# Tying the splits of the output projection's attention rows behind chosen exponentials and masked sums

## The chip, the cores and the metric

The kernel runs on one core of a Trainium2 chip. The metric is device time in microseconds (us) of one execution; several executions are timed and their median is taken. One more execution is taken by the hardware profiler, and all durations of single instructions come from it.

## What is computed

One block of a streaming encoder on 1024 rows of width 1024, all in float32: a SwiGLU feed-forward with a layer norm, a mixer with a layer norm, a second feed-forward with a layer norm. Cut to what matters here, the mixer:

```python
fox = forgetting_attention(q, k, v, fg)            # 8 heads of width 64, blocks of 128 queries
lru = gelu(z_lg) * rg_lru(conv(z_lx))              # 512 recurrent channels
mix = concat([fox, lru], -1) @ w_out               # 512 attention rows and 512 recurrent rows of w_out
x   = layer_norm(ALPHA * x + mix)
# attention, of each head and each block i of 128 queries, on the keys up to the diagonal:
s = q_i @ k.T * scale + cum[queries] - cum[keys];  s = where(mask, s, -1e30);  p = softmax(s);  o_i = p @ v
```

## The kernel before

A float32 matrix product is done in three passes: each operand is split into a high part in the format fp32r and a low part, the rest, and `mm3` (lines 156 to 158) adds high x high, high x low and low x high. A split is a cast by ScalarE (the high part) and a subtraction by VectorE (source minus high part).

The program is written with a framework that takes the instructions in program order with their dependencies and then chooses each engine's order itself: an instruction that is ready and has its buffers can be put ahead of earlier ones that are not ready. `issue_behind(later, earlier)` and `issue_after` give it an order to keep: `later` may not be put ahead of `earlier` on their common engine. Such a tie adds no semaphore.

The attention (`attention`, with `probs`, `to_pT` and `values`) runs over a list of 64 units, a unit being a head and a block i of 128 queries. Heads 0 to 5 go one after another, blocks 7 down to 0; the 16 units of heads 6 and 7 are interleaved, in the order (6,7) (6,6) (6,5) (6,4) (7,7) (7,6) (6,3) (6,2) and so on. So unit 40 is (5,7), unit 47 is (5,0), unit 48 is (6,7), unit 49 (6,6), unit 51 (6,4) and unit 53 (7,6). In the profile a unit is known by the width of its exponential, 128 x (i + 1) columns. For unit n:

- `probs`: the scores by TensorE (lines 999 and 1000) into one of two score buffers; GpSimd masks the diagonal of the `cum` tile (line 1003); VectorE adds `cum` and takes the minimum over the row in one instruction, the masked sum (line 1005); ScalarE takes the exponential (line 1006), which also adds up the row. For heads 0 to 3 the row is then divided by its sum (lines 1008 and 1009).
- `to_pT` of an earlier unit (three units back in the first four heads, two in the others): TensorE transposes the exponentials (line 1020), ScalarE and VectorE split them (lines 1024 and 1025).
- `values`, one unit later still, for each pair of blocks: TensorE multiplies by v (line 1041), ScalarE and VectorE take the result out (lines 1044 and 1045), and after the second head of a pair it is scaled (lines 1050 and 1051) and split into the mix tiles (lines 1053 and 1054).

Between the units stands other work. The recurrent half of the output projection, sixteen tiles of 12 matmuls (`fill`), goes into units 0 to 35. The attention half is done by the output tiles (`out_tile`), from unit 56 on, each of 12 matmuls and every second one followed by the layer norm of its rows; they need the mix tiles of four pairs of heads and the four split rows of `w_out`. These splits are made by the generator `out_w`, one for each `next(w_steps)`, and kept in `w_fox`. It loads two row blocks into one `raw` tile, then splits each by `split_ws` (lines 148 and 149). The parts go into `ws` tiles, eight buffers, which the splits of the recurrent rows hold before. The `raw` tiles have two buffers; after the attention the first weights of the second feed-forward take them (line 264, on SyncE's queue, where the loads of heads, of stored mix tiles (line 1110) and of the layer norm's two rows stand as well). The first use of those weights is at line 319.

Of the kernel before, what the change touches and what calls it, by code (L numbers as in the profile page):

```python
# [12 lines left out]
AF = mybir.ActivationFunctionType  # L13
ALU = mybir.AluOpType
# [34 lines left out]
def f32(ap):  # L49
    return ap.bitcast(F32)  # L50


class Block:
# [91 lines left out]
    def split_ws(self, src, k):  # L145

        hi, lo = (self.wsp.tile([P, 4 * VW], F32R, tag="ws", name=self.nm("w"))[:, 0:D].rearrange("p (k c) -> p k c", k=k) for _ in range(2))
        self.nc.scalar.copy(hi, src)
        self.nc.vector.tensor_tensor(lo, src, f32(hi), ALU.subtract)
        return hi, lo  # L150

    def mm3(self, out, lhs, rhs, first, last, goes_on=False):
# [810 lines left out]
    def attention(self, w_out, mixp, ln, normed):  # L963

        nc, v = self.nc, self.nc.vector
# [5 lines left out]
        with self.pool("att_p", 3) as pp, self.pool("att_t", 1) as tp, self.pool("att_pt", 6) as ptp, self.pool("att_qk", 2, side="right") as qkp:  # L971

            def load(h):
                vt = qkp.tile([P, NT, P], F32R, tag="v", name=self.nm("v"))
                cum = qkp.tile([P, T], F32, tag="cum", name=self.nm("cum"))
                q, kh, kl = (qkp.tile([P, T], F32R, tag=t, name=self.nm(t)) for t in ("q", "kh", "kl"))
                mine = slice(64 * (h % 2), 64 * (h % 2) + 64)
                for j in range(2):
                    rows = slice(64 * j, 64 * j + 64)
                    nc.sync.dma_start(f32(q[rows]), self.q_d[h // 2, j, mine, :])  # L980
                    nc.sync.dma_start(f32(kh[rows]), self.k_d[h // 2, 0, mine, :])
                    nc.sync.dma_start(f32(kl[rows]), self.k_d[h // 2, 1, mine, :])
                row = self.cum_d[h:h + 1, :]
                nc.sync.dma_start(cum, bass.AP(tensor=row.tensor, offset=row.offset, ap=[[0, P], [1, T]]))
                self.last_load = nc.sync.dma_start(f32(vt), self.v_d[h].rearrange("(j p) d -> p j d", p=P))
                return q, kh, kl, vt, cum

            sums, inv = self.fgz, self.wf.rearrange("p h i -> p (h i)").rearrange("p (h i) -> p h i", h=HEADS)

            def probs(h, i):  # L990

                q, kh, kl, _, cum = heads[h]
                n = (i + 1) * P
                ts = slice(i * P, n)
                s = self.s_tile()
                for bank in range((n + H - 1) // H):
                    c1 = min(max(n - bank * H, 256), H)
                    cols = slice(bank * H, bank * H + c1)
                    mm(s[:, bank, 0:c1], q[:, ts], kh[:, cols], start=True, stop=False)
                    scores = mm(s[:, bank, 0:c1], q[:, ts], kl[:, cols], start=False, stop=True)  # L1000
                sf = s.rearrange("p b c -> p (b c)")
                p = pp.tile([P, T], F32, tag="p", name=self.nm("p"))
                nc.gpsimd.affine_select(cum[:, ts], cum[:, ts], pattern=[[-1, P]], compare_op=ALU.is_ge, fill=1e30, base=0, channel_multiplier=1)
                m = self.small.tile([P, 4], F32, tag="m", name=self.nm("m"))
                v.tensor_tensor_reduce(p[:, 0:n], sf[:, 0:n], cum[:, 0:n], 1.0, 3e38, ALU.add, ALU.min, m[:, 1:2])
                nc.scalar.activation(p[:, 0:n], p[:, 0:n], AF.Exp, bias=m[:, 1:2], scale=-1.0, accum_out=sums[:, h, i:i + 1])
                if h < LAST:
                    v.reciprocal(m[:, 3:4], sums[:, h, i:i + 1])
                    nc.gpsimd.tensor_scalar(p[:, 0:n], p[:, 0:n], m[:, 3:4], 1.0, op0=ALU.mult, op1=ALU.mult)
                return p, scores  # L1010

            def to_pT(h, i, p):
                if i % 2:
                    pts[h, i // 2] = [tuple(ptp.tile([P, 4, 256], F32R, tag="pt", name=self.nm("pt")) for _ in range(2))
                                      for _ in range((i + 4) // 4)]
                for g in range((i + 4) // 4):
                    js = range(4 * g, min(4 * g + 4, i + 1))
                    pa = self.a_tile()
                    for j in js:
                        nc.tensor.transpose(pa[:, (j % 4) * P:(j % 4 + 1) * P], p[:, j * P:(j + 1) * P], self.ident)  # L1020
                    w = len(js)
                    pav = pa.rearrange("p (j t) -> p j t", j=4)[:, 0:w, :]
                    hi, lo = (x[:, 0:w, (i % 2) * P:(i % 2 + 1) * P] for x in pts[h, i // 2][g])
                    nc.scalar.copy(hi, pav)
                    v.tensor_tensor(lo, pav, f32(hi), ALU.subtract)
                if h > LAST and h % 2 and i % 2 == 0:
                    r = inv[:, h - 1:h + 1, i:i + 2]
                    v.reciprocal(r, sums[:, h - 1:h + 1, i:i + 2])
                    nc.gpsimd.tensor_copy(self.gate_raw.rearrange("p u (b d) -> p u b d", b=2),
                                          r.rearrange("p b u -> p u b").unsqueeze(3).to_broadcast([P, 2, 2, 64]))  # L1030
# [28 lines left out]
            heads, pts, ps, outs, mixes = {}, {}, {}, {}, {}  # L1059
# [9 lines left out]
            def due(n):  # L1069

                return [u for u in (n - AHEAD, n - AHEAD + 1) if 0 <= u < len(units) and u + AHEAD - (u >= LAST * NT) == n]
# [3 lines left out]
            def out_tile():  # L1075
                i, d = tiles.pop(0)
                self.down_tile(i, list(zip(mix + [mixes[3]], w_fox)), 1.0, (d,))
                if d:
                    self.layer_norm(i)
                    normed(i)  # L1080

            for n in range(len(units) + AHEAD + 1):
                if n < len(units):
                    h, i = units[n]
                    if i == 5 and h < 6 or (h, i) == (6, 6):
                        heads[h + 1] = load(h + 1)
                    if i == NT - 1:
                        if h % 2 == 0:
                            outs[h // 2] = tp.tile([P, T], F32, tag="o", name=self.nm("o"))
                        else:  # L1090
                            mixes[h // 2] = tuple(mixp.tile([P, T], F32R, tag="h", name=self.nm("mix")) for _ in range(2))
                    ps[n], scores = probs(h, i)
                for m in due(n):
                    to_pT(*units[m], ps.pop(m))
                for m in due(n - 1):
                    h, i = units[m]
                    if i % 2 == 0:
                        values(h, i // 2)
                        if h == HEADS - 1:
                            tiles += [(i + 1, 0), (i + 1, 1), (i, 0), (i, 1)]  # L1100
                if fill and (n < 2 or n % 8 in (2, 3, 4)):
                    i, d = fill.pop(0)
                    with self.tc.issue_after(scores.ins) if n < 3 else nullcontext():
                        self.down_tile(i, lru_tiles, 1.0, (d,))
                if 45 <= n < 53 and n % 2:
                    w_fox.append(next(w_steps))
                if n in MIXES:
                    mix.append(tuple(self.hp.tile([P, T], F32R, tag="h", name=self.nm("mix")) for _ in range(2)))
                    for l in range(2):
                        nc.sync.dma_start(f32(mix[-1][l]), mix_d[len(mix) - 1][l])  # L1110
                    if len(mix) == 3:
                        self.load_gb(*ln, [self.hp.tile([P, T], F32, tag="h", name=self.nm("gb")) for _ in range(2)])
                if tiles:
                    out_tile()
# [136 lines left out]
```

## Time and profile before

| what | value |
|---|---|
| median of three runs | 2323.7 us (2322.83 to 2324.29) |
| profiled execution, time | 2323.84 us |
| profiled execution, span | 2322.1 us |
| TensorE matmul, busy | 2302.8 us |
| VectorE, busy | 1631.8 us |
| ScalarE, busy | 1012.6 us |
| granted TensorE clock, mean | 0.999 |
| first and last exponential of the attention, start | 1184.5 and 1358.4 us |

Times in the profile are us from the start of the span. PE is TensorE (PEld its weight loads), DVE is VectorE, ACT is ScalarE, POOL is GpSimd, SPq the queue of DMA issues on SyncE. A line such as L1006 is line 1006 of the kernel before. In a time line the columns are start, duration, engine, line, operation, output and input by the program's names, shapes, count, and in brackets the idle time of the engine just before it and what ended it. In a row of instruction groups the three numbers are the shortest, the median and the longest duration in ns.

### The profile page before, as it was taken

How to read it: one execution, taken by the hardware profiler on the slowest of the kernel's cores; microseconds unless marked ns; L12 is line 12 of the kernel's file. 1: busy time of each engine (PE TensorE's matmuls, PEld its weight loads, DVE VectorE, ACT ScalarE, POOL GpSimd, SP SyncE). 2: the span in 40 equal slices, each digit the busy share in tenths (PEclk: the TensorE clock that was granted, in tenths of full speed). 3: DMA queues.
4: the chain of work that ended last, by engine and by line, in shares of the span. 5: the costliest groups of instructions: out<-in, count | busy, mean ns of one | idle time of the engine just before them, and what ended most of it. 6: DMA issues, size and time to landing. Idle time of an engine off the chain costs nothing.

```text
span 2322.1 us, 28275 instructions
## 1 busy us (share of the span) xinstructions
PE 2302.8 (99%) x10737; PEld 1916.8 (83%) x10737; DVE 1631.8 (70%) x2489; ACT 1012.6 (44%) x1589; POOL 202.7 (9%) x344
## 2 busy tenths in 40 slices
PE   9999999999999999999999999999999999999998
PEld 7888888888888888888898787888888888888887
DVE  8766566666567788866667899665656665577886
ACT  5443333333344335454456745434333333344342
POOL 0020000000000000111133200000000000000000
PEclk9999999999999999999999999999999999999999
DMA  4333232323375433132275812232323232564542
GB/s 145 129 94 119 87 118 87 118 87 118 125 265 200 163 127 120 65 103 96 101 203 146 245 64 94 88 118 88 122 93 124 87 118 87 193 246 169 182 144 73
DMA packets 175976, 298.93 MB, mean 129 GB/s; under 512 B 8208, under 2 KB 100688, under 8 KB 175840
## 3 DMA queue, kind: packets, MB, share of 16 engines
q1 hardware_dynamic: 152768, 218.16, 28.9%
q0 software_dynamic: 23072, 78.97, 8.6%
q8 instruction: 84, 1.38, 0.2%
q14 instruction: 52, 0.43, 0.1%
HBM read 214.22 MB, written 82.87 MB: 128 GB/s over the span
## 4 chain that ended last, share of the span: by engine, by line
PE 93%; DVE 4%; ACT 1%; DMA 1%; issue 1%; SPq 0%; DVEq 0%; ACTq 0%
PE x L156 9%; PE x L158 9%; PE x L157 9%; PE b L156 7%; PE b L157 7%; PE b L158 7%; PE s L157 6%; PE s L158 6%; PE s L156 6%; PE a L158 6%; PE a L156 6%; PE a L157 6%; PE a L1041 1%; PE a L1020 1%; PE a L898 1%
## 5 line engine op out<-in xcount | busy, mean ns | idle before, releaser
L283 ACT CAST ws<-t 128x512 fp32r<-128x512 f32 x240 | 149.1, 623 | 394.6 <-PE b L157 267.3
L283 ACT CAST ws<-raw 128x512 fp32r<-128x512 f32 x180 | 112.0, 623 | 258.2 <-PE x L157 256.8
L284 DVE TENSOR_TENSOR ws<-raw,ws 128x512 fp32r<-128x512 f32 x180 | 123.9, 688 | 141.3 <-ACT ws L283 137.9
L284 DVE TENSOR_TENSOR ws<-t,ws 128x512 fp32r<-128x512 f32 x240 | 164.5, 686 | 70.4 <-ACT ws L283 68.5
L156 PE MATMUL b<-As,ws 128*128 128x512 f32 x512 | 199.6, 390 | 0.8 <-ACT row L517 0.4
L157 PE MATMUL a<-ws,ws 128*128 128x512 f32 x512 | 199.6, 390 | 0.2
L156 PE MATMUL a<-ws,ws 128*128 128x512 f32 x512 | 199.3, 390 | 0.5 <-ACT row L526 0.5
L157 PE MATMUL b<-As,ws 128*128 128x512 f32 x512 | 199.5, 390 | 0.0
L156 PE MATMUL x<-As,ws 128*128 128x512 f32 x512 | 199.3, 389 | 0.0
L158 PE MATMUL b<-As,ws 128*128 128x512 f32 x512 | 199.3, 389 | 0.0
L158 PE MATMUL a<-ws,ws 128*128 128x512 f32 x512 | 199.2, 389 | 0.0
L158 PE MATMUL x<-As,ws 128*128 128x512 f32 x512 | 199.2, 389 | 0.0
L157 PE MATMUL x<-As,ws 128*128 128x512 f32 x512 | 199.2, 389 | 0.0
L156 PE MATMUL x<-A,ws 128*128 128x512 f32 x496 | 193.3, 390 | 0.1
L158 PE MATMUL x<-A,ws 128*128 128x512 f32 x496 | 193.1, 389 | 0.0
L157 PE MATMUL x<-A,ws 128*128 128x512 f32 x496 | 193.0, 389 | 0.0
L621 ACT CAST ws<-raw 128x1024 fp32r<-128x1024 f32 x112 | 117.4, 1050 | 159.3 <-PE a L157 88.1
L624 DVE TENSOR_TENSOR ws<-raw,ws 128x1024 fp32r<-128x1024 f32 x112 | 136.6, 1221 | 53.0 <-ACT ws L621 52.5
L556 POOL DMA_DIRECT2D h_d<-row x96 | 68.8, 719 | 1147.2 <-DVE row L550 1108.1
L156 PE MATMUL s<-ws,ws 128*128 128x512 f32 x384 | 149.5, 389 | 0.0
L158 PE MATMUL s<-ws,ws 128*128 128x512 f32 x384 | 149.4, 389 | 0.0
L157 PE MATMUL s<-ws,ws 128*128 128x512 f32 x384 | 149.4, 389 | 0.0
(255 smaller groups left out, 5210.5 us busy)
## 6 DMA issues: line engine op xcount, KB each, us to landing
raw<-h_d SPq DMA_DIRECT2D x56, 1024.0 KB, 5.4
h_d<-row POOLq DMA_DIRECT2D x96, 512.0 KB, 3.4
wd<-in_ffn_w_down_dram SPq DMA_DIRECT2D x32, 1024.0 KB, 7.6
raw<-in_ffn_w_gate_dram SPq DMA_DIRECT2D x30, 1024.0 KB, 5.1
raw<-in_ffn_w_up_dram SPq DMA_DIRECT2D x30, 1024.0 KB, 5.2
h_d<-row POOLq DMA_DIRECT2D x32, 256.0 KB, 2.4
raw<-in_w_in_dram SPq DMA_DIRECT2D x16, 512.0 KB, 4.7
row<-in_x_dram SPq DMA_DIRECT2D x12, 512.0 KB, 8.4
```

What stands on the lines that cost most here:

```text
L156: mm(out, ah, bh, start=first, stop=False, skip_group_check=goes_on)
L157: mm(out, ah, bl, start=False, stop=False, skip_group_check=goes_on)
L158: mm(out, al, bh, start=False, stop=last, skip_group_check=goes_on)
L283: nc.scalar.copy(hi, src)
L284: v.tensor_tensor(lo, src, f32(hi), ALU.subtract)
L556: nc.gpsimd.dma_start(d[:, 2 * n:2 * n + 2], t.rearrange("p (r t) -> p r t", r=2))
L621: cast = nc.scalar.copy(hi, src)
L624: self.mark = v.tensor_tensor(lo, src, f32(hi), ALU.subtract)
L898: nc.tensor.matmul(pa[:, 0:width], xh, wh[:, 0:width], start=k == 0, stop=False)
L1020: nc.tensor.transpose(pa[:, (j % 4) * P:(j % 4 + 1) * P], p[:, j * P:(j + 1) * P], self.ident)
L1041: mm(pv[:, ps], vt[:, j, :], pts[h, qt][j // 4][l][:, j % 4, ps], start=j == 0 and l == 0, stop=j == last and l == 1)
```

## The change

The splits of the attention rows of `w_out` are asked for two units later, at units 47, 49, 51 and 53 instead of 45, 47, 49 and 51. And each is given two ties: its cast goes behind the exponential of that unit on ScalarE, its subtraction behind the masked sum of that unit on VectorE. For that, `split_ws` keeps its two instructions, and `probs` returns the exponential and the masked sum.

```diff
     def split_ws(self, src, k):
...
-        self.nc.scalar.copy(hi, src)
-        self.nc.vector.tensor_tensor(lo, src, f32(hi), ALU.subtract)
+        self.split_ops = (self.nc.scalar.copy(hi, src),
+                          self.nc.vector.tensor_tensor(lo, src, f32(hi), ALU.subtract))
...
-                v.tensor_tensor_reduce(p[:, 0:n], sf[:, 0:n], cum[:, 0:n], 1.0, 3e38, ALU.add, ALU.min, m[:, 1:2])
-                nc.scalar.activation(p[:, 0:n], p[:, 0:n], AF.Exp, bias=m[:, 1:2], scale=-1.0, accum_out=sums[:, h, i:i + 1])
+                low = v.tensor_tensor_reduce(p[:, 0:n], sf[:, 0:n], cum[:, 0:n], 1.0, 3e38, ALU.add, ALU.min, m[:, 1:2])
+                exp = nc.scalar.activation(p[:, 0:n], p[:, 0:n], AF.Exp, bias=m[:, 1:2], scale=-1.0, accum_out=sums[:, h, i:i + 1])
...
-                return p, scores
+                return p, scores, (exp, low)
...
-                    ps[n], scores = probs(h, i)
+                    ps[n], scores, ops = probs(h, i)
...
-                if 45 <= n < 53 and n % 2:
+                if 47 <= n < 55 and n % 2:
                     w_fox.append(next(w_steps))
+                    for part, op in zip(self.split_ops, ops):
+                        self.issue_behind(part, op)
```

## The prediction

> **What bounds the kernel now.** I read the page first, then a table of busy time by stretch through attention, the chain that ended last around the four splits, the time lines of TensorE, ScalarE and VectorE there, and last SyncE's queue and the uses of the raw tiles.
>
> ```profile
> span 2322.1 us, 28275 instructions
> PE 2302.8 (99%) x10737; PEld 1916.8 (83%) x10737; DVE 1631.8 (70%) x2489; ACT 1012.6 (44%) x1589; POOL 202.7 (9%) x344
> ...
> PE 93%; DVE 4%; ACT 1%; DMA 1%; issue 1%; SPq 0%; DVEq 0%; ACTq 0%
> ```
>
> TensorE is the bound of the whole. Only 7% of the chain lies off it, so a change on ScalarE and VectorE can matter only where TensorE waits for them. The next table is of the stretches that the splits leave and enter.
>
> ```profile
> core 0: us, PE busy (x) PEld busy (x) DVE busy (x) ACT busy (x) POOL busy (x), PEclk, DMA share, GB/s
> 1271.30:1281.50 10.20, 10.19 (x58) 8.75 (x59) 9.27 (x19) 9.13 (x19) 1.83 (x6) 1.00 0.62 153
> 1281.50:1292.45 10.95, 10.20 (x75) 9.09 (x73) 10.36 (x24) 8.18 (x20) 1.74 (x5) 1.00 0.82 286
> 1292.45:1308.30 15.85, 14.79 (x97) 11.82 (x96) 14.38 (x38) 13.10 (x34) 5.09 (x12) 1.00 0.98 246
> 1308.30:1328.60 20.30, 19.41 (x137) 16.38 (x137) 18.49 (x42) 17.42 (x40) 6.80 (x17) 1.00 0.92 290
> 1328.60:1345.00 16.40, 16.03 (x88) 13.20 (x87) 13.43 (x31) 8.49 (x19) 2.71 (x6) 1.00 0.25 96
> ```
>
> The first stretch still holds matmuls of the recurrent rows, which fill TensorE (10.19 of 10.20 us). They end at 1281.5 us. The first output tile starts at 1328.6 us. Between the two TensorE has attention alone, and VectorE is busy 10.36 of 10.95, 14.38 of 15.85 and 18.49 of 20.30 us (95, 91 and 91%): it is the engine that sets the pace there. From 1328.6 us TensorE is covered again and VectorE has air (13.43 of 16.40). The granted clock is 1.00 in every stretch, so no part of the argument hangs on it.
>
> **Where the splits stand now.** First the rows of the two split lines in this stretch and the shares of the chain from 1279.5 to 1289 us, then ScalarE's time line, then TensorE's.
>
> ```profile
> L148 ACT CAST w<-raw x4: 1046/1050/1061, 1279.6 to 1288.3; 128x1024 fp32r<-128x1024 f32 x4
> L149 DVE TENSOR_TENSOR w<-raw,w x4: 1217/1220/1226, 1280.7 to 1293.8; 128x1024 fp32r<-128x1024 f32 x4
> by line: ACT w L148 32.4%; ACT p L1006 14.3%; DVE w L149 12.9%; ACT pt L1024 11.3%; issue 10.8%; ACT o L1044 7.7%; DVE row L222 7.3%; DVE p L1005 6.3%; DVE mix L1054 3.5%; DVE m L1005 0.2%; ACTq L1006 0.2%; DVEq L1005 0.0%
> ```
>
> ```profile
> 1284.65 1.05 ACT L148 CAST w<-raw 128x1024 fp32r<-128x1024 f32 x1
> 1285.72 0.37 ACT L1044 COPY o<-a 64x256 f32<-64x256 f32 x1
> 1286.11 0.58 ACT L1024 CAST pt<-a 128x512 fp32r<-128x512 f32 x1
> ```
>
> ```profile
> 1285.71 0.65 PE L1020 MATMUL a<-ident,p 128*128 128x128 f32 x4
> 1286.75 0.39 PE L1041 MATMUL a<-pt,v 128*128 128x256 f32 x1 [0.39 <-ACT pt L1024]
> ...
> 1289.88 0.48 PE L999 MATMUL s<-kh,q 128*128 128x512 f32 x1
> 1290.72 0.39 PE L1041 MATMUL a<-pt,v 128*128 128x256 f32 x1 [0.37 <-ACT pt L1024]
> ...
> 1293.14 0.28 PE L1000 MATMUL s<-kl,q 128*128 128x256 f32 x1
> 1293.79 1.09 PE L1020 MATMUL a<-ident,p 128*128 128x128 f32 x8 [0.37 <-ACT p L1006]
> ```
>
> The program asks for the splits at units 45 to 51, but the scheduler has put all four casts between 1279.6 and 1288.3 us, among units 35 to 40, as soon as the weight buffers of the recurrent rows come free. In that stretch 32.4% and 12.9% of the chain, some 4.3 of 9.5 us, are splits. The reader should see the cast of 1284.65 (1.05 us) with the copy and the cast of line 1024 queued behind it on ScalarE, and TensorE waiting for that last one at 1286.75; the second wait follows the last split cast (1288.3) in the same way, the third follows the subtractions that delay unit 40's masked sum.
>
> **The change part by part.** No instruction is added or dropped: the same 4 casts and 4 subtractions, the same two loads of the raw rows. Keeping the two handles in `split_ws` and returning them from `probs` issues nothing. The ties carry no semaphore; they fix order on one engine. What moves:
>
> (1) *The early stretch is freed.* The lost TensorE time is the start of the stalled matmul less the start before it and its pitch. The pitches are estimates from the rows above: 0.11 us for a transpose (four in 0.65, less a tail of 0.2), 0.12 and 0.23 for 256 and 512 columns (durations of 0.28 and 0.39 less the same overlap of about 0.16). So 1286.75 - 1285.71 - 0.44 = 0.60; 1290.72 - 1289.88 - 0.23 = 0.61; 1293.79 - 1293.14 - 0.12 = 0.53. Together 1.74 us, and since each follows a split I take all of it as given back. The ends are 0 (VectorE's other load sets the pace and a new wait takes the place of each) and 2.05 us (the 1.74 and 0.1 for each restart of the weight pipeline).
>
> (2) *The late stretch is loaded.* Unit 47 is the last of head 5, 49 the second of head 6, 51 the fourth, 53 the second of head 7. The first and the last of their exponentials, and the long gaps of VectorE behind them:
>
> ```profile
> 1304.95 0.40 ACT L1006 ACTIVATE p<-p,m 128x128 f32<-128x128 f32 x1
> ...
> 1321.24 1.05 ACT L1006 ACTIVATE p<-p,m 128x896 f32<-128x896 f32 x1 [0.22 <-DVE m L1005]
> ```
>
> ```profile
> 1306.56 0.42 DVE L1045 TENSOR_TENSOR o<-o,a 64x256 f32<-64x256 f32 x1 [0.76 <-ACT o L1044]
> ...
> 1319.78 0.41 DVE L1045 TENSOR_TENSOR o<-o,a 64x256 f32<-64x256 f32 x1 [0.77 <-ACT o L1044]
> ...
> 1329.44 0.18 DVE L1028 RECIPROCAL wfr<-fgz 128x4 f32<-128x4 f32 x1 [1.05 <-ACT p L1006]
> ```
>
> A split can start at the earliest behind these, so all four land between 1305.3 and about 1325 us, in the stretches with VectorE at 91%. Four subtractions are 4 x 1.22 = 4.88 us of VectorE. The casts run on ScalarE beside that, so they are not added again. Behind a subtraction the next unit's masked sum is queued, and behind that the exponential, the transposes and the release of the score banks. The three long gaps, 0.76 + 0.77 + 1.05 = 2.58 us, can swallow part: 4.88 - 2.58 = 2.3 us, which I take, because in the early stretch, with splits in it, VectorE's idle time is down to 10.95 - 10.36 = 0.59 us, so gaps do get filled. The ends are 0 (the subtractions run while TensorE has its own work) and 4.88 (they meet no gap).
>
> (3) *Who waits for the weights.* The first output tile starts at 1328.6 us and takes them in order, and the last split is done at about 1321.24 + 1.05 + 1.05 + 1.22 = 1324.6 us: 4 us early. Nothing; were the cover gone, TensorE would wait at line 156.
>
> (4) *SyncE's queue.* The raw tiles are two buffers, and the next to use them are the first weights of the second feed-forward block.
>
> ```profile
> 1313.37 0.46 SPq L264 DMA_DIRECT2D raw<-in_ffn_w_up_dram  x1
> ...
> 1321.69 1.56 SPq L1110 DMA_DIRECT2D mix<-mix_d  x2
> L319 ACT CAST ws<-raw x4: 603/618/624, 1369.8 to 1389.1; 128x512 fp32r<-128x512 f32 x4
> DMA to landing us min/median/max: 4.9/6.1/9.3
> ```
>
> The gate loads now wait for split 2 and the up loads for split 4 (1324.6 instead of 1313.4, 11 us later). With 9.3 us to landing that is 1334 us, 36 us before the first use at 1369.8. Cost nothing, unless the up load stands in the queue ahead of the mix pair now at 1321.69: a rival below. The two loads of the raw output rows are asked for two units later, long before use: nothing.
>
> The sum: -1.74 + 2.3 = +0.56, so +0.6 us. Against the profiled execution (2323.84 us with a span of 2322.1) 2324.4; the median of the three runs, 2323.7, lies 0.14 below that execution, so 2324.3. What a measurement of this kernel can tell from no change is about 0.2%, 4.65 us.
>
> **A lock between VectorE and GpSimd.** The subtraction's two inputs are both in SBUF, and the trace shows what that does:
>
> ```profile
> 1293.81 1.22 DVE L149 TENSOR_TENSOR w<-raw,w 128x1024 fp32r<-128x1024 f32 x1
> 1293.96 1.22 POOL L1003 TENSOR_SCALAR_AFFINE_SELECT cum<-cum 128x128 f32<-128x128 f32 x1 [1.20 <-DVE m L1005]
> L1003 POOL TENSOR_SCALAR_AFFINE_SELECT cum<-cum x53: 283/292/1221, 1200.7 to 1332.8; 128x128 f32<-128x128 f32 x53
> ```
>
> The mask of the next unit took 1.22 instead of 0.292 us, and ended at 1295.18, 0.15 us behind the subtraction. A mask starts when the masked sum before it is done, the very instruction behind which the subtractions are now tied, so all four may hold one: 4 x 0.15 = 0.6 us more on the way to the next masked sum. The Trainium skill, "SBUF — State Buffer", section "Who interferes with whom", has the rule: a VectorE instruction with two SBUF inputs and a GpSimd instruction that reads SBUF exclude each other for the whole instruction. By that rule the sum would be +1.2 us; the trace agrees in the one overlap it shows, by 1.22 against 0.292.
>
> **The rivals.** *The gain is kept* (33%): the subtractions fall into gaps, term (2) goes to 0, and 2323.7 - 1.74 gives 2322.0, down to 2321.65. For it: the early splits are on the chain, and the late stretch has the 2.58 us of gaps. Against: two of the three gaps end when ScalarE's copy comes, and a cast put in front of that copy makes the gap longer instead of filling it.
>
> *VectorE pays in full* (7%): each subtraction stands between two masked sums, no gap is met, and a wait comes back early for each one removed: 4.88 + 0.6 = +5.5, 2329.2 us, slower by 0.24%. It decides as soon as the subtractions start right where VectorE has other work ready and TensorE's score banks are both taken. For it: VectorE at 91% in that stretch and TensorE's waits there on masked sums. Against: 1.74 us of early waits can hardly all return.
>
> *The mix pair waits in SyncE's queue* (5%): if the up load is ordered first, the pair goes out at 1324.6 + 0.46 instead of 1321.69, 3.4 us later. It decides only past the slack, the third weight of the first tile, some 2 us behind 1328.6; so +0.6 + 1.4 at the worst, 2325.7 us, and with the normalisation's two rows, which go out behind the pair, up to the whole 3.4, 2327.7 us. Against: the queue's order is chosen with the buffers' release known.
>
> *The ties change nothing* (3%): not possible by order, since the units they name run at 1305 us and later; only the splits going even further back, under the output tiles, would give 2322.0 to 2323.7.
>
> **How the numbers follow.** The forecast, 2324.3, has 52%, with a range of its own from 2323.0 to 2326.3 (a late cost of 1.0 to 4.3 against the same 1.74). The range over all cases is 2321.5 to 2327.5: it takes in the kept gain and the queue's rival nearly whole and leaves out the full price. Faster by over 0.2% would need more than the 2.05 us bound: 2%. Slower by over 0.2% needs the full price or a large part of it beside the queue: 5%. Within 0.2%: 93%.
>
> **What would show it.** Right if the casts and subtractions of the split lie at 1305 to 1326 us in the profile after, the waits at 1286, 1290 and 1293 shrink or go, and TensorE's waits on masked sums between 1305 and 1328 grow; the first output tile should then start within 1 us of 1328.6. Term (1) is wrong if unit 40's exponential still starts at 1292.5; term (2) if the stretch from head 6's first exponential to the first output tile keeps its 20.3 us. Wrong altogether if the scheduler reorders the attention units around the freed places, so that their order on TensorE no longer compares.

## The result, and the profile after

The changed kernel takes 2327.8 us (median of 20 runs, 2326.1 to 2331.06) against 2323.57 us before (20 runs, 2321.94 to 2325.7): ratio 1.0019, 95% interval 1.0013 to 1.0025. It is slower by 4.2 us. The profiled execution took 2328.62 us with a span of 2326.9 us.

The page of the profile after, its span, engines and chain; below it, the table by stretch for the same five stretches as before.

```profile
span 2326.9 us, 28267 instructions
...
PE 2302.3 (99%) x10737; PEld 1915.4 (82%) x10737; DVE 1631.8 (70%) x2489; ACT 1012.6 (44%) x1589; POOL 203.1 (9%) x344
...
PE 92%; DVE 4%; DMA 1%; ACT 1%; issue 1%; SPq 0%; POOL 0%; DVEq 0%; POOLq 0%; ACTq 0%
```

```profile
1271.30:1281.50 10.20, 10.20 (x60) 8.62 (x59) 8.60 (x19) 7.10 (x16) 2.02 (x6) 1.00 0.60 152
1281.50:1292.45 10.95, 10.94 (x80) 9.81 (x79) 8.73 (x23) 7.65 (x22) 1.66 (x6) 1.00 0.82 290
1292.45:1308.30 15.85, 13.36 (x91) 11.06 (x90) 12.68 (x33) 12.26 (x30) 4.58 (x11) 1.00 1.05 254
1308.30:1328.60 20.30, 17.16 (x114) 13.69 (x113) 18.81 (x37) 18.05 (x37) 6.73 (x14) 1.00 0.75 238
1328.60:1345.00 16.40, 14.50 (x83) 11.95 (x82) 11.85 (x31) 7.76 (x18) 2.86 (x7) 1.00 0.31 107
```

TensorE's work is the same (2302.3 against 2302.8 us), so the whole loss is idle time of TensorE. In the second stretch it is now busy 10.94 instead of 10.20 us, in the last three 13.36, 17.16 and 14.50 instead of 14.79, 19.41 and 16.03. To see where, I measure distances between the starts of four landmarks: the first score matmul of the attention, the exponentials of units 45 (384 columns), 47 (128) and 53 (896), and the first matmul of an output tile. The rows of before (first) and after (second); those of units 47 and 53 of before stand in the prediction.

```profile
1177.30 0.62 PE L999 MATMUL s<-kh,q 128*128 128x512 f32 x2
1302.32 0.62 ACT L1006 ACTIVATE p<-p,m 128x384 f32<-128x384 f32 x1
1328.63 0.48 PE L156 MATMUL a<-w,mix 128*128 128x512 f32 x1
```

```profile
1176.71 0.62 PE L999 MATMUL s<-kh,q 128*128 128x512 f32 x2
1300.11 0.62 ACT L1006 ACTIVATE p<-p,m 128x384 f32<-128x384 f32 x1
1304.32 0.40 ACT L1006 ACTIVATE p<-p,m 128x128 f32<-128x128 f32 x1
1324.03 1.04 ACT L1006 ACTIVATE p<-p,m 128x896 f32<-128x896 f32 x1
1333.61 0.48 PE L156 MATMUL a<-w,mix 128*128 128x512 f32 x1
```

| stretch | before | after | difference |
|---|---|---|---|
| attention's start to unit 45 | 125.02 | 123.40 | -1.62 |
| 45 to 47 | 2.63 | 4.21 | +1.58 |
| 47 to 53 | 16.29 | 19.71 | +3.42 |
| 53 to the first output tile | 7.39 | 9.58 | +2.19 |

The sum is +5.57. The attention began 0.59 us earlier in the execution after, before any changed instruction, and 0.2 us come back behind the first tile: 5.57 - 0.59 - 0.2 = 4.8 us, the difference of the spans. So there are one gain and three losses. The gain is the one that the prediction's first step describes.

**The second loss is the one that was meant: the splits.** First the four long waits of TensorE between units 48 and 53 after, then VectorE's rows of the first split, of the masked sum of unit 51 and of the last split:

```profile
1311.03 1.09 PE L1020 MATMUL a<-ident,p 128*128 128x128 f32 x8 [0.49 <-ACT p L1006]
1314.97 0.50 PE L999 MATMUL s<-kh,q 128*128 128x512 f32 x1 [0.58 <-DVE m L1005]
1316.71 1.95 PE L1020 MATMUL a<-ident,p 128*128 128x128 f32 x13 [0.66 <-DVE pt L1025]
1319.36 0.50 PE L999 MATMUL s<-kh,q 128*128 128x512 f32 x1 [0.70 <-DVE m L1005]
```

```profile
1305.79 1.23 DVE L149 TENSOR_TENSOR w<-raw,w 128x1024 fp32r<-128x1024 f32 x1 [0.59 <-ACT w L148]
1307.04 0.42 DVE L1045 TENSOR_TENSOR o<-o,a 64x256 f32<-64x256 f32 x1
...
1314.09 0.82 DVE L1005 CUSTOM_DVE_ANT_0 p<-s,cum 128x640 f32<-128x640 f32 x1 [1.23 <-POOL cum L1003]
...
1326.14 1.23 DVE L149 TENSOR_TENSOR w<-raw,w 128x1024 fp32r<-128x1024 f32 x1
```

The reader should see that VectorE stood idle 0.59 us for the cast before it could subtract: cast and subtraction come in series there, with the addition of line 1045 and the masked sum of unit 48 behind both. TensorE's second wait (1314.97) is for a masked sum that had itself waited 1.23 us for a mask of GpSimd, so not every wait in this stretch stands straight behind a split. And the last split comes behind unit 53's exponential (1324.03): only three of the four lie between the exponentials of units 47 and 53, the fourth lies in the next stretch.

**The first loss is at unit 46, the first step past unit 45.** The rows after, from SyncE, GpSimd, VectorE and TensorE:

```profile
1278.93 11.35 SPq L1112 DMA_DIRECT2D mix<-mix_d  x4
...
1294.12 0.53 SPq L984 DMA_DIRECT2D cum<-cum_d  x1
```

```profile
1302.21 0.54 POOL L1003 TENSOR_SCALAR_AFFINE_SELECT cum<-cum 128x128 f32<-128x128 f32 x2 [3.91 <-DMA cum<-cum_d]
```

```profile
1302.78 0.42 DVE L1005 CUSTOM_DVE_ANT_0 p<-s,cum 128x256 f32<-128x256 f32 x1 [1.63 <-POOL cum L1003]
```

```profile
1303.27 0.50 PE L999 MATMUL s<-kh,q 128*128 128x512 f32 x1 [1.54 <-DVE m L1005]
```

GpSimd runs its masks in a fixed order. That order has a mask of head 6's `cum` tile ahead of the one that unit 46 needs, and head 6's tile lands at 1302.2 us, because SyncE is held for 11.35 us, as before, by the loads of stored mix tiles. Before, the same mask came at 1302.51 us behind a wait of 2.00 us, and the work that needed its successor came hardly earlier: 45 to 47 took 2.63 us there, against 2.52 in a kernel without that wait (e8). Counted from the attention's start the tile is there at 125.2 us before and 125.5 us after. So head 6's transfer is a wall that does not move: what arrives 1.6 us earlier waits there.

**The third loss is at the first output tile.** GpSimd's rows of before, then after, then TensorE's after:

```profile
1323.99 0.40 POOL L1029 COPY gate_raw<-wfr 128x256 f32<-128x256 f32 x1
1326.06 0.29 POOL L1003 TENSOR_SCALAR_AFFINE_SELECT cum<-cum 128x128 f32<-128x128 f32 x1 [1.67 <-DVE m L1005]
1331.01 1.04 POOL L185 TENSOR_SCALAR gb<-gb 128x1024 f32<-128x1024 f32 x1 [4.66 <-DMA gb<-in_ln_g_dram]
```

```profile
1331.72 1.04 POOL L185 TENSOR_SCALAR gb<-gb 128x1024 f32<-128x1024 f32 x1 [5.96 <-DMA gb<-in_ln_g_dram]
1332.73 0.28 POOL L1003 TENSOR_SCALAR_AFFINE_SELECT cum<-cum 128x128 f32<-128x128 f32 x1
1332.97 0.39 POOL L1029 COPY gate_raw<-wfr 128x256 f32<-128x256 f32 x1
```

```profile
1333.41 0.44 PE L1050 MATMUL a<-ident,gate_raw 128*128 128x128 f32 x2 [1.84 <-POOL gate_raw L1029]
```

Line 185 prepares a row of the layer norm (`load_gb`; I call it the negation) and waits for that row's transfer. Before, the copy of line 1029 and the mask came ahead of it; after, it stands ahead of both, and 5.96 us of waiting for a transfer hold a copy of 0.39 us that TensorE needs. The scheduler reordered GpSimd around the moved splits, although no instruction of GpSimd was changed. Built with the later units but without the ties, the program has the order of the kernel before on every engine; with ties on the four casts alone it has that of the changed kernel. So the casts' ties are the whole change. (Neither of these two programs was timed.) TensorE's own order changed with them as well: the scores keep their order, but transposes and value products stand in other places between them. The kernel before and e7 below differ from each other in this way too, at units 47 to 49, and both take 16.3 us from 47 to 53; the order of the changed kernel was not timed without its splits, so its share in the second loss stays open.

### The profile page after: what moved, and what is told of

It is laid out like the page before. It is cut to its first block, busy times and chain, and to the rows that moved or that the text cites. A ratio compares the mean times of both kernels' runs of the same rounds, so it can differ in the third digit from the quotient of the medians.

```text
span 2326.9 us, 28267 instructions
## 1 busy us (share of the span) xinstructions
PE 2302.3 (99%) x10737; PEld 1915.4 (82%) x10737; DVE 1631.8 (70%) x2489; ACT 1012.6 (44%) x1589; POOL 203.1 (9%) x344
## 4 chain that ended last, share of the span: by engine, by line
PE 92%; DVE 4%; DMA 1%; ACT 1%; issue 1%; SPq 0%; POOL 0%; DVEq 0%; POOLq 0%; ACTq 0%
PE x L156 9%; PE x L158 9%; PE x L157 9%; PE b L157 7%; PE b L156 7%; PE b L158 7%; PE s L158 6%; PE s L157 6%; PE s L156 6%; PE a L156 6%; PE a L158 6%; PE a L157 6%; PE a L1041 1%; PE a L1020 1%; PE a L898 1%
```

## The experiments

Theory A says that the three losses are separate causes: the late splits, the wait at head 6's tile, and the negation in GpSimd's order. Theory B is the prediction's rival, VectorE paying for four subtractions. Medians are against the kernel before as run on the same chip: 2323.83 us (29 runs) beside the first four, 2323.78 (33) beside the next four, 2323.88 (33) beside the last four. Their 95% intervals are about 0.0009 wide to each side, 2 us, so pieces of 1 to 2 us are read from the distances of the profiled executions, in the table behind the experiments.

**e1: the negation behind the gate copy.** `load_gb` only keeps the negation, and it is issued at n == 56 with a tie.

```diff
-        self.nc.gpsimd.tensor_scalar(gb[0], ...)
+        self.negate = lambda: self.nc.gpsimd.tensor_scalar(gb[0], ...)
...
-                if tiles:
+                if n == 56 and self.issue_behind(self.negate(), self.gate_copy) or tiles:
```

> The changed kernel with one difference in GpSimd's order alone: the negation of the layer norm's gain row (line 185) stands behind the copy of the reciprocals for the first output rows (line 1029) instead of two masks and a copy ahead of it. Theory A (three pieces: the late splits cost about 3 us, GpSimd's queue costs TensorE 2.0 us in front of the first output tile, and the early gain of 2 us is lost at a wait for head 6's cum tile): TensorE's wait of 1.84 us for the copy of line 1029 goes, the first output tile starts 1.5 to 2.0 us earlier, near 1331.8, and the time falls to about 2326.0. Theory B (VectorE pays for the four subtractions in full, the wait on GpSimd is only where that delay shows): another wait takes its place and the time stays within 0.5 us of 2327.8.

Measured 2329.14 us, ratio 1.0023 (1.0014 to 1.0032). The first tile no longer waited at its start (53 to tile 7.54 instead of 9.58 us), but the time did not fall: the negation now stood ahead of unit 57's mask, and TensorE waited inside the first tile.

```profile
1332.86 1.05 POOL L185 TENSOR_SCALAR gb<-gb 128x1024 f32<-128x1024 f32 x1 [2.60 <-DMA gb<-in_ln_g_dram]
1333.88 0.29 POOL L1003 TENSOR_SCALAR_AFFINE_SELECT cum<-cum 128x128 f32<-128x128 f32 x1
```

```profile
1336.50 0.50 PE L156 MATMUL a<-w,mix 128*128 128x512 f32 x1 [2.84 <-ACT mix L1053]
```

**e2: the second mix pair behind the loads of heads 6 and 7**, on SyncE; only that queue's order differs from the changed kernel.

```diff
-                        nc.sync.dma_start(f32(mix[-1][l]), ...)
+                        with self.tc.issue_after(self.last_load.ins) if n == 50 else nullcontext(): nc.sync.dma_start(f32(mix[-1][l]), ...)
```

> The changed kernel with one difference in SyncE's order alone: the loads of the second stored mix pair stand behind the loads of heads 6 and 7 instead of ahead of them. Theory A: SyncE no longer holds head 6's loads until 1290.4 us while it waits for the mix pair, the cum tile of head 6 lands some 3 us earlier, VectorE's wait of 1.63 us for the mask in front of unit 46 goes, and the early gain is kept to the late stretch: 1.0 to 1.8 us faster than the changed kernel, about 2326.4. Theory B: the late stretch is paced by VectorE's load, an earlier start only makes another wait longer: within 0.5 us of 2327.8. A later landing of the second mix pair would show as a wait of the first output tile.

Measured 2330.01 us, 1.0026 (1.0015 to 1.0037). The wall is gone, 45 to 47 falls from 4.21 to 2.52 us, and yet the time does not fall: 53 to the first tile grew to 10.45 us. The negation ended at 1333.08 us (after: 1332.76). Counted from the attention's start that is 0.9 us earlier, not 1.7, so TensorE waited longer for the copy behind it, 2.57 instead of 1.84 us; and half the clock followed (below), with 994.2 instead of 993.3 us from the first tile to the end.

**e3: both of them.**

> The changed kernel with both differences of queue order: line 185 behind the copy on GpSimd, the second mix pair behind the loads of heads 6 and 7 on SyncE. Theory A: the two gains add to 2.5 to 3.8 us, about 2324.5, and what is left against the kernel before is the late splits' cost less the early gain, 0.5 to 1.5 us. Theory B: within 1 us of 2327.8.

Measured 2328.97 us, 1.0023 (1.0014 to 1.0032). 45 to 47 took 2.52, 53 to tile 7.52 us, but with the same hole as e1 behind the first tile's start: a wait of 1.54 us for the mix tile. A waiting instruction moved half way only changes whom it holds. The profiled execution, 2326.6 us, was the fastest of the eleven; what makes the median 2.4 us longer is not shown. In e1, e2 and e3 neither theory's number came out. All three medians lie above that of the changed kernel, but by no more than the intervals.

**e4: no splits.** From the changed kernel, the four splits and their two loads left out, the recurrent weights standing in, without the moves of e1 and e2.

```diff
-                    w_fox.append(next(w_steps))
-                    for part, op in zip(self.split_ops, ops):
-                        self.issue_behind(part, op)
+                    w_fox.append(lru_tiles[len(w_fox)][1])
```

> The changed kernel without the four splits and without the two loads of the attention rows of the output weights: the split recurrent rows stand in for them in the output tiles. Theory A: the early stretch is as in the changed kernel (wait in front of unit 46 included, 1.6 us), the late stretch is free of 4.88 us of subtractions and 4.2 us of casts, and line 185 falls behind the copy in GpSimd's order by itself: 2322.0 to 2323.0, so 1 us under the kernel before and 5 to 6 us under the changed one. Theory B (nothing but the subtractions): 4.9 us under the changed kernel, 2322.9. The place of the remaining waits tells more than the time here.

Measured 2323.66 us, 0.9999 (0.9990 to 1.0008), above both theories' numbers: with no split at all it is no faster than before. 45 to 47 took 4.31 us, the wall again. The negation fell back behind the copy and the mask by itself, as A had said (53 to tile 7.41 us). Behind the wall stood a stretch at half the clock, told below, which makes 47 to 53 17.62 us; but the profiled execution, 2326.49 us, was the slowest of the eleven, so the median is not explained by it.

**e5: the negation behind unit 57's mask**, like e1 with `n == 57` and the tie to the mask of line 1003.

> The changed kernel with one instruction moved in GpSimd's order: the negation of line 185, which waits for a transfer until about 1331.7 us, stands behind the mask of unit 57, so that neither the gate copy nor the last large mask has to wait for it. Theory A (three pieces: 3.4 us of late splits, 2.0 us at this negation, the early gain of 2.2 us lost at head 6's wait): no wait at the start of the first output tile and none behind it, the tile starts 2 to 3 us after that of the kernel before, the time is 2325.5 to 2326.0 us, ratio to before 1.0008 to 1.0011. Theory B (VectorE pays in full for four subtractions): the masked sums of the last head are as late as ever, the tile starts 4.5 to 5 us after, 2327.5 to 2328.5 us. Theory C (beside A; TensorE idle for more than about 2.1 us within one window of 3.413 us brings half the clock for the next window, up to 1.7 us): with the wait of 1.84 us gone the half-clock stretch is seldom and the highest time is nearer to the lowest than the 5 us of the changed kernel.

Measured 2326.55 us (2325.59 to 2327.9), 1.0012 (1.0003 to 1.0021). GpSimd now runs the mask first:

```profile
1331.71 0.29 POOL L1003 TENSOR_SCALAR_AFFINE_SELECT cum<-cum 128x128 f32<-128x128 f32 x1 [0.39 <-DVE m L1005]
1332.09 1.04 POOL L185 TENSOR_SCALAR gb<-gb 128x1024 f32<-128x1024 f32 x1
```

TensorE's time line shows no wait for GpSimd at the first tile or behind its start. 53 to tile is 7.52 us, 2.06 less than in the changed kernel. The time is 0.55 us above Theory A's range and below Theory B's.

**e6: e5 with e2's move.**

> As the run before it, and the loads of the second pair of mix rows stand in SyncE's order behind the loads of heads 6 and 7, so that the sums of head 6 are in place before unit 46 needs them. Theory A: the step from unit 45's exponential to unit 46's is 1.5 us instead of 3.2, the early gain of about 2 us is kept, the first tile starts 0 to 1.2 us after that of the kernel before without a wait: 2323.7 to 2324.9 us, ratio 1.0001 to 1.0006. Theory B: the gain at unit 46 is eaten by the subtractions, since VectorE is full: 2326 to 2328 us. Theory C: no window with more than 2.1 us of TensorE idle from unit 45 on, so no half clock there and a scatter as narrow as that of the kernel before.

Measured 2325.72 us (2324.8 to 2326.78), 1.0007 (0.9999 to 1.0016). 45 to 47 is 2.51 us, 1.9 less than in e5, while the medians differ by 0.8. What is left against the kernel before is the splits' price less the early gain. It lies between the ranges of A and B, 0.8 us above A's.

**e7: e6 without the splits** (e4's edit).

> As the run before it, but without the four splits and the two loads of their rows: the output projection multiplies the recurrent weights' tiles instead, so the work of TensorE is the same. This is what the attention stretch takes when no split is in it and neither queue stands in the way. Theory A: the early gain of 2.2 us without a late cost: 2321.3 to 2322.0 us, ratio 0.9990 to 0.9994, and the difference to the run before it, 2.5 to 3.5 us, is the price of four splits in the late stretch. Theory B: the difference is 4.9 us or more, so the run before it stands at 2326 us or above.

Measured 2321.79 us, 0.9991 (0.9982 to 1.0000). By medians four late splits cost 3.9 us, more than A's 2.5 to 3.5 and less than B's 4.9. Against e4, which lies 1.9 us higher, the wall is gone: 45 to 47 is 2.51 instead of 4.31 us. By distances, 47 to 53 is 16.26 us without splits (first) and 19.70 with them (e6, second), and 53 to the first tile 7.41 and 7.53. So the three splits in the first of these stretches cost 3.44 us, the fourth next to nothing:

```profile
1302.49 0.41 ACT L1006 ACTIVATE p<-p,m 128x128 f32<-128x128 f32 x1
...
1318.75 1.05 ACT L1006 ACTIVATE p<-p,m 128x896 f32<-128x896 f32 x1 [0.22 <-DVE m L1005]
```

```profile
1302.57 0.42 ACT L1006 ACTIVATE p<-p,m 128x128 f32<-128x128 f32 x1
...
1322.27 1.04 ACT L1006 ACTIVATE p<-p,m 128x896 f32<-128x896 f32 x1
```

**e8: the kernel before with both moves of the queues.**

> The kernel before, its splits where they were, with the two moves in the queues (negation behind unit 57's mask, second mix pair behind the loads of heads 6 and 7). Theory A: its early waits last until unit 46 anyway, so head 6's wait is short there and the negation stood late already: within 0.7 us of the kernel before, 2323.0 to 2323.9 us, ratio 0.9997 to 1.0001. Were the two moves worth by themselves what they are worth in the changed kernel (some 3.5 us), it would be 2320 to 2321 us, and the queues would be a fault of their own with nothing to do with the splits.

Measured 2323.34 us, 0.9998 (0.9990 to 1.0007): as A said. The two queues cost the kernel before next to nothing; they cost only a kernel that arrives early at the one and is reordered at the other.

**e9 and e10: half a split each**, from e6; the low (e9) or the high part (e10) of the recurrent weights stands in.

> The kernel with both queue moves (2325.7 us with four splits, 2321.8 without), of each split only ScalarE's cast, tied as before; the four subtractions are left out and the recurrent weights' low tiles stand in. Theory A1 (the price of 3.9 us is VectorE's: each subtraction of 1.22 us stands ahead of the next masked sum): 2322.0 to 2322.8 us, nearly the time without splits. Theory A2 (the price is ScalarE's: each cast of 1.05 us stands ahead of a copy that VectorE's addition and TensorE's banks wait for): 2324.5 us or more. The order of a few attention matmuls differs by the scheduler's choice in this kernel and the next, so differences under 0.5 us decide nothing.

> The counterpart: of each split only VectorE's subtraction (from the loaded rows, the recurrent weights' high tiles standing in for the casts, which are left out). Theory A1: 2324.8 to 2325.7 us, nearly all of the 3.9 us. Theory A2: 2322.0 to 2323.2 us. If casts and subtractions are both dear, or only the two together, both runs lie between 2323 and 2325 us or their prices do not add up to 3.9 us.

Measured 2323.89 us for the casts alone and 2323.02 us for the subtractions alone: 2.1 and 1.2 us above e7. Neither A1 nor A2 (e10 lies in A2's range, e9 in none), but the third case: both parts are dear. The distances agree. The exponentials of units 47 and 53 with casts only, then with subtractions only:

```profile
1303.34 0.41 ACT L1006 ACTIVATE p<-p,m 128x128 f32<-128x128 f32 x1
...
1321.33 1.06 ACT L1006 ACTIVATE p<-p,m 128x896 f32<-128x896 f32 x1
```

```profile
1303.92 0.41 ACT L1006 ACTIVATE p<-p,m 128x128 f32<-128x128 f32 x1
...
1322.09 1.05 ACT L1006 ACTIVATE p<-p,m 128x896 f32<-128x896 f32 x1
```

17.99 and 18.17 us, so 1.73 and 1.91 over the 16.26 of e7; together 3.64, and with whole splits it is 3.44. From unit 45 to the first tile, where all four stand, it is 2.17 us for the casts, 1.44 for the subtractions and 3.56 for whole splits, nearer to the medians. VectorE's idle time from 47 to 53 tells how: 2.2 us in the kernel before and in e7, 0.2 with subtractions only, 3.8 with casts only, 2.1 with both. Alone, the subtractions fill the gaps; with their casts they do not. Some matmuls of the attention stand in another order in e7, e9 and e10 than in e6, so the two shares are good to some tenths.

**e11: only the third and fourth split tied**, the first two falling back beside units 35 and 36 (`... if n > 49 else ():` behind the `zip`).

> The kernel with both queue moves, and only the third and fourth split tied; the first two fall back to where the kernel before has them (beside units 35 and 36). If the price goes by the split (late 3.9/4 = 0.98 us, early 1.55/4 = 0.39 us, from the runs with both moves: 2325.72 and 2323.34 against 2321.79): 2321.8 + 0.8 + 1.95 = 2324.5 us, within 0.5. If instead one pair carries the late price, 2323 or 2325.5 us.

Measured 2323.72 us, 0.9992 (0.9983 to 1.0001), below the expected 2324.5. Some matmuls stand ahead of unit 47 here that stand behind it in e6 (45 to 47 is 3.48 us with no wait in it), so the row of the table below is read by its sum up to the first tile: 151.2 us, as in e8 with all four early (151.2), against 149.9 in e7 and 153.1 in e6. A price by the split would have put it halfway between e8 and e6, at 152.1. Two late splits cost no more than the same two early; four late cost two and a half times as much as four early (3.25 against 1.28 us over e7). Of the two, one lies between 47 and 53, which takes 16.59 us: 0.33 more than without splits, where three had cost 3.44. So the price is not a fixed one by the split.

**e12: third and fourth split at units 54 and 56**, from e11 (`if n in (47, 49, 54, 56):`).

> As the run before it, but the third and fourth split tied behind units 54 and 56, at the end of head 7's first units, where the first output tile begins to cover TensorE. Theory A: a split costs only where TensorE has nothing but attention, so the two cost less there than at 51 and 53: 2321.8 + 0.8 + 0 to 1.2 = 2322.6 to 2323.8 us, the best of the versions that compute everything. Rival: the first tile asks for its third weight some 2.5 us after its start, the fourth split is not ready, TensorE waits at line 156, and with more than about 2.1 us of idle in one window the half clock comes on top: 2325 us or more.

Measured 2324.0 us, 0.9997 (0.9988 to 1.0005), 0.2 us above A's range. 47 to 53 is free of splits (16.26 us), but 53 to the first tile takes 8.54 instead of 7.41 us. The price has only moved into the next stretch, and it is no lower there: up to the first tile e12 takes 151.8 us, e11 151.2.

| run | start to 45 | 45 to 47 | 47 to 53 | 53 to tile | tile to end | median |
|---|---|---|---|---|---|---|
| before | 125.0 | 2.63 | 16.29 | 7.39 | 993.5 | 2323.57 |
| after | 123.4 | 4.21 | 19.71 | 9.58 | 993.3 | 2327.8 |
| e1 negation half way | 123.4 | 3.96 | 19.72 | 7.54 | 997.8 | 2329.14 |
| e2 mix pair later | 123.5 | 2.52 | 19.71 | 10.45 | 994.2 | 2330.01 |
| e3 e1 and e2 | 123.4 | 2.52 | 19.72 | 7.52 | 995.0 | 2328.97 |
| e4 after, no splits | 124.4 | 4.31 | 17.62 | 7.41 | 993.0 | 2323.66 |
| e5 negation behind 57 | 123.4 | 4.42 | 19.70 | 7.52 | 993.2 | 2326.55 |
| e6 e5 and e2 | 123.4 | 2.51 | 19.70 | 7.53 | 993.3 | 2325.72 |
| e7 e6, no splits | 123.7 | 2.51 | 16.26 | 7.41 | 993.7 | 2321.79 |
| e8 before, queues | 125.1 | 2.52 | 16.20 | 7.39 | 992.9 | 2323.34 |
| e9 casts only | 123.4 | 2.51 | 17.99 | 7.85 | 993.3 | 2323.89 |
| e10 subtractions only | 123.4 | 2.51 | 18.17 | 6.94 | 993.1 | 2323.02 |
| e11 two late | 123.6 | 3.48 | 16.59 | 7.54 | 993.6 | 2323.72 |
| e12 at 54 and 56 | 123.6 | 3.49 | 16.26 | 8.54 | 993.2 | 2324.0 |

The third column of distances is the clearest reading: 19.70 to 19.72 in all six kernels with all four splits late, three of them in this stretch, and 16.20 to 16.29 in four of the five that have none in it (e4's half clock is the fifth). No version that computes everything is measurably faster than the kernel before; the best median, e8's, is within its interval.

## Why the prediction was wrong

The forecast was +0.6 us and the measurement +4.2 us. The prediction had also held that under 0.2% nothing could be told from no change; with twenty runs of each kernel the interval is 0.06% to each side, so the 0.19% is clear of it. Step by step:

- **(1) The early stretch is freed: right.** -1.74 us forecast, -1.62 measured to unit 45. Unit 40's exponential starts at 1290.58 instead of 1292.49 us, which is 1.3 us earlier when counted from the attention's start. What failed is that I let the gain run on to the end. A wall stood 6 units later: GpSimd's mask for head 6 had a wait of 2.00 us for a transfer already before. It stands in the same time line of GpSimd as the mask of 1293.96 us that the prediction shows, and I gave it no term. With it moved (e5 to e6) 45 to 47 fell from 4.42 to 2.51 us.
- **(2) The late stretch is loaded: too small by a half.** 2.3 us forecast, 3.56 measured (e6 against e7, unit 45 to the first tile). The step that failed is the sentence "The casts run on ScalarE beside that, so they are not added again": casts alone cost 1.73 us from 47 to 53 (e9). For the subtractions alone the model of the gaps was near. In that stretch it gives three of them less the two gaps there, 3.66 - 1.53 = 2.13 us, and they cost 1.91 (e10). What it missed is that the casts keep the gaps open: with both parts VectorE's idle time there stays at 2.1 us. The prediction had the reason itself, as its argument against the kept gain: a cast put in front of ScalarE's copy makes the gap longer. That e11's two late splits cost no more than two early ones may be because two subtractions, 2.44 us, are still under the 2.58 us of gaps; that is argued, not shown.
- **(3) Who waits for the weights, (4) SyncE's queue: right.** No wait at line 156 for a split. The mix pair went out at 1322.30 us instead of 1321.69, the up loads behind it at 1327.39. But the first output tile started at 1333.61 us, 5 us behind 1328.6 and not within 1 us of it, which was one of the prediction's signs of being right.
- **The lock of VectorE and GpSimd: seen, but not on the path.** Two of the four subtractions held a GpSimd instruction:

```profile
1305.85 1.42 POOL L1029 COPY gate_raw<-wfr 128x256 f32<-128x256 f32 x1 [1.56 <-PE a L1050]
...
1314.99 1.46 POOL L1003 TENSOR_SCALAR_AFFINE_SELECT cum<-cum 128x128 f32<-128x128 f32 x2 [0.94 <-DVE m L1005]
```

  1.42 instead of the 0.40 us of that copy elsewhere, and 1.46 instead of the 0.54 us of two masks. The rule cited in the prediction agrees with both rows. The 0.6 us that I put beside it is not seen: no instruction is shown waiting for either.
- **What was missing altogether: GpSimd's own order.** I asked what each queue is moved past for SyncE, and not for GpSimd, although line 185 with 4.66 us of waiting for a transfer stood there before. It is worth 2.06 us at the tile (e5). This and the wall of (1) are what carried the time past the forecast's own range of 2323.0 to 2326.3 us: e6, with the early gain and the late splits but neither block, took 2325.72 us.

Nearest in size was the far end of the mix pair's rival, 2327.7 us, and that is luck: it needs the pair and the layer norm's rows to leave 3.4 us late, behind the up load, and they left 0.6 us late, ahead of it. The rival that gave 2329.2 us had 4.88 us of subtractions where there were 3.56 us of whole splits, and returned waits where there were two blocked queues.

By medians, each against the kernel before as run beside it, the two queues together account for 2.3 us (the changed kernel +4.2, e6 +1.9) and the splits for 3.9 (e6 to e7); e7 lies 2.0 us under the kernel before, most of it the price of the early splits (e8 to e7: 1.55). 3.9 + 2.3 - 2.0 = 4.2. By the distances up to the first tile the same three are 3.77, 3.25 and 1.45 us, and 3.77 + 3.25 - 1.45 is the +5.57 from above. So the three pieces are shown, but their sizes only to about 1.5 us.

## What to carry to other kernels

A gain upstream is worth only as much as the next wait that does not move with it: follow it to the first instruction that waits for a transfer, on every engine's queue, GpSimd's too, and see who stands behind. When a scheduler orders the engines, a tie on one engine can reorder another, so compare the orders of all of them before costing the edit. Where the engine that paces a stretch waits for a second one in series, as here a subtraction for its cast, both durations have to be costed.

## What the runs showed of the hardware

The clock was not expected to come into it. In three profiled executions the granted clock fell within the attention or the output tiles to one half, for one stretch of 3.41 us, each time just behind a stretch of that length in which TensorE had been busy for about half or less. The tables by stretch, columns as above with the granted clock third from the end: of e4, of e1, of e2 and, without a fall, of the changed kernel.

```profile
1303.57:1306.98 3.41, 1.76 (x11) 1.33 (x10) 1.61 (x8) 1.75 (x7) 1.88 (x5) 1.00 1.11 317
1306.98:1310.40 3.42, 3.42 (x18) 3.24 (x17) 1.34 (x4) 1.15 (x4) 0.40 (x1) 0.50 1.04 220
```

```profile
1334.00:1337.40 3.40, 0.90 (x3) 0.55 (x4) 2.46 (x6) 1.32 (x3) 0.86 (x3) 1.00 0.06 22
1337.47:1340.88 3.41, 3.41 (x11) 2.81 (x10) 1.84 (x3) 0.48 (x1) 0.00 (x0) 0.50 0.00 0
```

```profile
1329.86:1333.27 3.41, 1.30 (x12) 1.16 (x10) 1.15 (x3) 1.40 (x3) 1.23 (x2) 1.00 1.00 374
1333.27:1336.68 3.41, 2.95 (x8) 2.46 (x9) 2.29 (x6) 1.33 (x3) 1.35 (x5) 0.50 0.27 96
```

```profile
1301.17:1304.59 3.42, 1.88 (x12) 1.46 (x11) 1.70 (x8) 1.87 (x7) 1.88 (x5) 1.00 1.12 308
1304.59:1308.00 3.41, 3.09 (x22) 2.44 (x20) 2.76 (x6) 2.34 (x6) 1.42 (x1) 1.00 1.04 217
```

1.76, 0.90 and 1.30 us busy were followed by half the clock, 1.88 was not. The 2.1 us of idle time in the expectations of e5, e6 and e12 matches e2's stretch (3.41 - 1.30); e4's shows that 1.65 us is enough, and the changed kernel's that 1.54 is not. In e4 the fall cost 17.62 - 16.26 = 1.36 us, and the longest wait ahead of it was 1.65 us.

The Trainium skill, "TensorE: Matmul & The Clock Gate", has the free-running window of 3413 ns (section "What's actually happening") and, under "HAM oscillation — how this bites in real kernels", the rule that idle gaps over about 3.4 us must be avoided. The window agrees. The gap does not: a wait of 1.65 us in e4, one of 2.57 in e2 and one of 2.84 in e1 were enough. Nor did the length of one gap decide, since the wait of 1.84 us in the changed kernel brought no fall (1331.90 to 1335.30 us: 1.89 of 3.40 us busy).

The fall may be why the runs of the changed kernel and of e1 to e4 scatter over 3.9 to 5.3 us and those of e5 to e12 over 1.7 to 3.0, but that stays open: no experiment set the length of a wait by itself, and single runs of the kernel before, whose profile shows no such stretch, went up to 2329.54 us as well. The runs' mean clocks point the same way: beside e9 to e12, the 24 runs of the kernel before with a mean of 0.999 took at most 2325.07 us, the five above 2326 us had 0.997 or 0.998. The loss itself does not come from the clock: the 14 runs of the changed kernel with 0.999 have a median of 2327.6 us.
